# Attention of a two-layer trunk: weighted sums in unbroken blocks of five key chunks, denominators at the blocks' heads, more tiles for exponentials, TensorE in written order

## The chip, the cores and the metric

The kernel runs on one core of a Trainium2 chip. The metric is device time in microseconds (us) of one execution; the time before is the median of three runs. The profile is one further execution, recorded instruction by instruction. Its engines are PE (TensorE matmuls), PEld (TensorE weight loads), DVE (VectorE), ACT (ScalarE), POOL (GpSimd) and SP (the queue that issues DMAs).

## What is computed

Two layers over 1024 latent and 256 context tokens of width 1024, all in float32. Each layer is a token mixer and a gated feed-forward part with a convolution; layer 0 mixes by grouped-query attention with normed and rotated heads, layer 1 by latent attention. Only the attentions matter here:

```python
def attend(q, k, v):                      # layer 0, 16 heads of 64; context queries attend to context keys alone
    s = jnp.einsum('bqhgd,bkhd->bhgqk', q, k) * scale
    p = softmax_f32(s).astype(v.dtype)
    return jnp.einsum('bhgqk,bkhd->bqhgd', p, v)
...
def attend(qn, qr, kn, kr, v):            # layer 1, 16 heads, 64 + 32 wide keys
    s = (jnp.einsum('bqhd,bkhd->bhqk', qn, kn) + jnp.einsum('bqhd,bkd->bhqk', qr, kr)) * scale
    p = softmax_f32(s).astype(v.dtype)
    return jnp.einsum('bhqk,bkhd->bqhd', p, v)
```

## The kernel before

**Tiles.** Attention works on *units*: a pair of heads and 512 queries. A layer has 16 units of 10 key chunks of 128 keys. For a chunk, `scores` (L628) writes the scores of both heads, transposed (keys on partitions), into one PSUM tile `psD` of 1024 columns: four matmuls in layer 0, six in layer 1, since operands are split into a high and a low part. ACT takes their exponential into a tile `pp` (shown as `pp<-psD`, 128x1024). `weigh` (L635) multiplies it with the values and adds into a PSUM tile `psB`: one matmul for each head, 128 keys by 64 value columns, the first head's result on partitions 0 to 63 and the second's on 64 to 127 (`tp`). These are plain float32 matmuls, and the trace has two MATMUL rows for each (640 of them make its 1280 rows). The sum of exponentials, the *denominator*, is collected in a tile `acc` by 128x1024 additions on POOL; in each unit chunk 4's tile is kept aside (`PAIRS`) and added to chunk 5's tile on DVE, and POOL adds the pair. `tail` (L640) copies the weighted sum out of PSUM, multiplies `acc` with a column of ones (`psB<-s,ones`, again 64 columns for each head), takes the reciprocal on DVE and multiplies.

**Maxima.** Exponentials need a bound for each query. `unit_max` (L589) computes the scores once more with queries on partitions (per unit 16 matmuls of 512 columns and 8 of 256, `psB<-blk,s`), and DVE reduces each bank (`mx<-psB`), 24 groups in 20 steps. A small chain on DVE (`m<-mx`, `mm<-m`, `mm<-m,mm`) and eight tiny matmuls (`psB<-identb,mm`) turn the result into a row, which two ACT copies put into the operands of the unit's scores (`s<-psB 2x512`). The unit's first score can be finished only then.

**Order.** An `Emitter` (L101) keeps an estimated clock of TensorE. The main stream (scores and weighted sums) advances it; side streams (preparing operands two units ahead, maxima, tails, the second layer's modulation, context queries in layer 0) run as generators that name a time to wait before the next step. `PACE0` and `PACE1` are the waits between steps of maxima. `em.until` runs side streams alone until a condition holds, here that the next unit's row of maxima is ready. What is written in this order is then ordered anew for each engine by a scheduler, except where an engine is pinned; in the attentions none is. Each engine runs its own instructions strictly in that final order.

**The main loop** (`Attention.run`, L704). After every two chunks (`BATCH`) `flush` writes the weighted sums of two earlier chunks and, behind each, its addition to `acc`. There are four `pp` tiles, seven `s4` tiles, two `psD` tiles and four `psB` tiles. Weight tiles `whi` and `wlo` (three each) hold the split weights.

## Time and profile before

| | us |
|---|---|
| median of 3 runs (lowest, highest) | 3500.96 (3500.63, 3502.84) |
| span of the profiled execution, first to last instruction | 3497.9 |
| median less span: what lies around the span | 3.1 |
| PE busy | 3328.7 |
| DVE, POOL, ACT busy | 2198.5, 1896.6, 1518.4 |
| attention of layer 0, about | 285 to 860 |
| attention of layer 1, about | 1990 to 2650 |

A row of instruction groups has the line, engine and operation, output and inputs by the program's names, shapes and count, then busy time and mean duration in ns, then idle time before it. All compute instructions have line L159, the helper that records them, so groups are told apart by their tiles. A timeline row has start, duration, and how many equal instructions were merged in it. Matmuls overlap: a row lasts longer than the time until the next one starts, so what a matmul costs is read from start to start. The profile names tiles `s` for `s2` and `s4`.

### The profile page before, as it was taken

The numbers are of one execution on the slowest core, as the hardware profiler recorded it, in microseconds if no ns is written. First come the engines' busy times: TensorE is split into PE (matmuls) and PEld (weight loads), VectorE is DVE, ScalarE is ACT, GpSimd is POOL, SyncE is SP. The second block draws the span as 40 slices with busy tenths as digits, with TensorE's granted clock in tenths as the row PEclk, the third lists the DMA queues.
The fourth block names the chain that finished last, engine by engine and source line by source line (L and its number), as shares of the span: only waits on it lengthen the run. The fifth ranks groups of instructions, "written<-read, shape, count | busy, mean of one in ns | idle before, by whom it ended". The sixth has DMA issues, their size and how long they took to land. (4 is left out here: it accounts for less than half of the span.)

```text
span 3497.9 us, 41426 instructions
## 1 busy us (share of the span) xinstructions
PE 3328.7 (95%) x15482; PEld 2337.4 (67%) x15482; DVE 2198.5 (63%) x2619; ACT 1518.4 (43%) x2328; POOL 1896.6 (54%) x1126
## 2 busy tenths in 40 slices
PE   6999999999989999999998899999999899999988
PEld 4666444445868888878887655555557677777777
DVE  5356677774477666765845645555664766676575
ACT  4234445543254444444444434343442444444434
POOL 4324656774276666654443355555562656665455
PEclk9999999999989999999999999999999899999999
DMA  5655310000302222245231100000013122223733
GB/s 195 198 152 182 131 37 8 8 31 7 136 32 95 85 76 83 95 143 192 86 121 65 37 25 14 26 12 26 19 48 120 50 97 97 91 91 106 243 106 106
DMA packets 139049, 303.31 MB, mean 87 GB/s; under 512 B 15584, under 2 KB 35168, under 8 KB 138848
## 3 DMA queue, kind: packets, MB, share of 16 engines
q1 hardware_dynamic: 138848, 300.67, 25.5%
q8 instruction: 121, 1.98, 0.2%
q14 instruction: 80, 0.66, 0.1%
HBM read 224.85 MB, written 70.52 MB: 84 GB/s over the span
## 5 line engine op out<-in xcount | busy, mean ns | idle before, releaser
L159 DVE TENSOR_REDUCE mx<-psB 128x1 f32<-128x512 f32 (+1 forms) x640 | 431.0, 686 | 346.4 <-PE psB L159 342.3
L159 POOL TENSOR_TENSOR s<-s,pp 128x1024 f32<-128x1024 f32 x216 | 518.2, 2399 | 184.9 <-DVE pp L159 140.0
L159 ACT ACTIVATE pp<-psD 128x1024 f32<-128x1024 f32 x320 | 327.1, 1024 | 394.3 <-PE psD L159 369.3
L159 PE MATMUL psD<-s,blk 128*128 128x512 f32 (+2 forms) x1600 | 475.5, 407 | 3.9 <-POOL s L159 2.7
L159 PE MATMUL psB<-pp,blk 128*64 128x512 f32 (+2 forms) x1424 | 465.8, 592 | 0.0
L159 PEld LDWEIGHTS psD<-s,blk 128*128 128x128 f32 (+2 forms) x1600 | 291.0, 190 | 176.8 <-issue 103.1
L159 PE MATMUL psD<-blk,wh 128*128 128x512 f32 (+1 forms) x1024 | 333.8, 402 | 7.4 <-ACT blk L159 3.9
L159 DVE SCALAR_TENSOR_TENSOR s<-s,par,s 128x1023 f32<-128x1023 f32 x176 | 286.3, 1639 | 70.2 <-ACT s L159 66.7
L159 DVE TENSOR_TENSOR s<-s,s 128x512 f32<-128x512 f32 (+3 forms) x233 | 256.7, 1102 | 90.7 <-ACT s L159 79.1
L159 PE MATMUL psD<-blk,wlo 128*128 128x512 f32 (+1 forms) x1398 | 289.1, 355 | 24.8 <-POOL wlo L159 24.8
L159 POOL TENSOR_TENSOR wl<-wr,wh 128x1024 fp32r<-128x1024 f32 (+3 forms) x58 | 105.1, 1811 | 349.6 <-ACT wh L159 335.4
L159 PE MATMUL psB<-blk,s 128*128 128x512 f32 (+3 forms) x768 | 277.3, 396 | 2.5 <-DVE mx L159 1.0
L159 PEld LDWEIGHTS psD<-blk,wlo 128*128 128x128 f32 x1398 | 229.8, 190 | 72.1 <-POOL wlo L159 33.5
L159 PE MATMUL psD<-blk,pp 128*128 128x512 f32 (+1 forms) x1068 | 267.1, 394 | 11.3 <-ACT s L159 5.5
L159 PE MATMUL psB<-blk,pp 128*128 128x512 f32 x1056 | 261.6, 395 | 6.2 <-DVE s L159 2.5
L159 PEld LDWEIGHTS psB<-blk,s 128*128 128x128 f32 (+1 forms) x768 | 138.7, 190 | 192.7 <-DVE mx L159 104.1
L159 DVE TENSOR_TENSOR pp<-pp 128x512 fp32r<-128x512 f32 (+1 forms) x165 | 139.7, 851 | 182.0 <-ACT pp L159 179.9
L159 POOL TENSOR_TENSOR pp<-wraw,pp 128x512 fp32r<-128x512 f32 x88 | 144.2, 1639 | 189.8 <-ACT pp L159 181.8
L159 PEld LDWEIGHTS psD<-blk,wh 128*128 128x128 f32 (+1 forms) x1024 | 188.7, 188 | 72.9 <-issue 20.0
L159 PEld LDWEIGHTS psD<-blk,pp 128*128 128x128 f32 x1068 | 199.5, 191 | 54.6 <-ACT s L159 6.6
L159 POOL TENSOR_TENSOR s<-s,s 128x1024 f32<-128x1024 f32 (+4 forms) x72 | 142.3, 1982 | 169.8 <-ACT s L159 145.6
L159 PEld LDWEIGHTS psB<-blk,pp 128*128 128x128 f32 x1056 | 198.3, 190 | 53.4 <-DVE s L159 6.3
(156 smaller groups left out, 6195.4 us busy)
## 6 DMA issues: line engine op xcount, KB each, us to landing
pp<-g SPq DMA_DIRECT2D x143, 256.0 KB, 2.7
g<-s SPq DMA_DIRECT2D x66, 512.0 KB, 2.7
s<-in_ada_w SPq DMA_DIRECT2D x48, 512.0 KB, 6.6
blk<-in_ada_w SPq DMA_DIRECT2D x48, 512.0 KB, 5.8
wraw<-in_w_up SPq DMA_DIRECT2D x88, 256.0 KB, 2.8
pp<-in_w_up SPq DMA_DIRECT2D x88, 256.0 KB, 3.4
blk<-in_w_dn SPq DMA_DIRECT2D x86, 256.0 KB, 3.1
wr<-in_w_out SPq DMA_DIRECT2D x16, 512.0 KB, 3.7
```

Of the source, the lines that this page charges most:

```text
L159: ins = fn(*a, **k)
```

## The change

- **Blocks.** `BATCH` becomes 5, with `LEAD` 2: when seven chunks are waiting, the weighted sums of five are written in one piece. While they are written, side streams are held back (`alone`), so nothing comes between them. Denominators, and the context queries' weighted sums, are not written where their stream stands, but queued (`post`) and written ahead of the next block (`run_jobs`).
- **TensorE pinned.** During `run`, `pinned` holds "pe": TensorE keeps the written order.
- **Additions.** They are written right behind the exponential. The pair of chunks 4 and 5 is gone; instead chunk 5 is added straight to `acc` by DVE (`ACCD`). POOL has eight additions a unit, as before, and DVE one.
- **Tiles.** Exponentials use `ptile`: 12 tiles in turn in layer 0 (six `pp`, three `whi`, three `wlo`), nine in layer 1 (six `pp`, three `wlo`). For that, narrow weights of layer 1 keep both parts in one `whi` tile, and the output projection's weights of layer 0 are loaded only at the last unit. `s4` gets eight tiles. The scratch for dynamic DMAs is set to 2048.
- **Small things.** The negated maximum (`mm<-m`) goes from DVE to ACT; paces are 0.55 and 0.75; the context queries' exponentials lie in one `blk` tile.

The diff also deletes comments; that part is left out.

```diff
-TAIL_WAIT = 4.0
-PACE0 = 0.8
+PACE0 = 0.55
...
-BATCH = 2
+BATCH = 5
+LEAD = 2
...
-PACE1 = 0.9
+PACE1 = 0.75
...
-PAIRS = (4,)
+ACCD = (5,)
...
     def _run(self):
-        if self.running:
+        if self.running or self.held:
             return
...
+    @contextmanager
+    def alone(self):
+        assert not self.held
+        self.held = True
+        yield
+        self.held = False
+        self._run()
...
-        return bp.tile([P, 1024], dt, tag="s4", name=nm("s4"), bufs=7)
+        return bp.tile([P, 1024], dt, tag="s4", name=nm("s4"), bufs=8)
...
-        return bp.tile([P, 1024], dt, tag="pp", name=nm("pp"), bufs=4)
+        return bp.tile([P, 1024], dt, tag="pp", name=nm("pp"), bufs=6)
+
+    def ptile():
+        tag, pool_, n = ptags["order"][ptags["next"] % len(ptags["order"])]
+        ptags["next"] += 1
+        return pool_.tile([P, 1024], F32, tag=tag, name=nm("pt"), bufs=n)
...
-            lo = wp.tile([P, 1024], F32R, tag="wlo", name=nm("wl"))
+            if w <= 512 and order[i][0] != "m_rope":
+                hi, lo = hi[:, 0:512], hi[:, 512:1024]
+            else:
+                lo = wp.tile([P, 1024], F32R, tag="wlo", name=nm("wl"))
...
-        dve.tensor_scalar(mb[:, :w, 0], m[:, :w], -1.0, None, ALU.mult)
+        act.mul(mb[:, :w, 0], m[:, :w], -1.0)
...
+    def run_jobs():
+        while jobs:
+            jobs.pop(0)()
+
+    def post(job):
+        if gather[0]:
+            jobs.append(job)
+        else:
+            job()
...
-        yield wait
-        pss = pB()
-        for h in range(2):
-            mm(pss[64 * h:64 * h + 64, :nq], ones, acc[:, h * nq:(h + 1) * nq], tp=(0, 64 * h))
+        res = {}
+
+        def total():
+            pss = res["pss"] = pB()
+            for h in range(2):
+                mm(pss[64 * h:64 * h + 64, :nq], ones, acc[:, h * nq:(h + 1) * nq], tp=(0, 64 * h))
+
+        post(total)
+        while not res:
+            yield 0.3
+        yield 1.0
...
+            gather[0] = True
+            pinned.add("pe")
 
             def flush(n):
-                for _ in range(min(n, len(pend))):
-                    weighted(*pend.pop(0))
-
-            def weighted(u, po, pt, i, last):
-                weigh(u, po, pt, i, i == 0, last)
+                with em.alone():
+                    run_jobs()
+                    for _ in range(min(n, len(pend))):
+                        u, po, pt, i = pend.pop(0)
+                        if i == 0:
+                            po[0] = pB()
+                        weigh(u, po[0], pt, i, i == 0, i == 9)
+                        if i == 9:
+                            em.spawn(tail(u, po[0], u["acc"]))
+
+            def add(u, pt, i):
                 if i == 0:
                     u["p0"] = pt
                 elif i == 1:
                     u["acc"] = s4()
                     pool.tensor_tensor(u["acc"], u.pop("p0"), pt, ALU.add)
-                elif i in PAIRS:
-                    u["pair"] = pt
                 else:
-                    if "pair" in u:
-                        dve.tensor_tensor(pt, pt, u.pop("pair"), ALU.add)
-                    eng = dve if u is self.units[-1] and i in LASTDVE else pool
+                    eng = dve if i in (LASTDVE if u is self.units[-1] else ACCD) else pool
                     eng.tensor_tensor(u["acc"], u["acc"], pt, ALU.add)
...
                 for k in range(10):
                     S = pD()
                     scores(u, S, k)
-                    pt = pp()
+                    pt = ptile()
                     act.activation(pt, S, AF.Exp, scale=self.scale)
-                    if len(pend) == BATCH:
+                    add(u, pt, k)
+                    pend.append((u, po, pt, k))
+                    if len(pend) == BATCH + LEAD:
                         flush(BATCH)
...
+            while pend:
+                flush(BATCH)
+            pinned.discard("pe")
+            gather[0] = False
+            run_jobs()
...
+    wide_tags = [("pp", bp, 6), ("whi", wp, 3), ("wlo", wp, 3)]
+    ptags.update(next=0, order=[t for k in range(6) for t in wide_tags if k < t[2]])
     att.run(ctx_side)
```

What this does to the order is seen at three places in the later part of layer 0's attention. TensorE before, around the row of maxima of one unit: `psD` are scores, `psB_1112` is the unit's weighted sum, `pp_1135` and `pp_1144` are two chunks' exponentials, `psB_1141` and `psB_1143` are maxima, `mm` is the row.

```order
L159 MATMUL psD_1145_5287<-s4_982_4675,blk_807_3999 128x512
L159 MATMUL psD_1145_5287<-s4_983_4676,blk_806_3998 128x512
L159 MATMUL psB_1141_5273<-blk_1052_4938,s4_1062_4970 128x512
L159 MATMUL psD_1145_5287<-s4_983_4676,blk_807_3999 128x512
L159 MATMUL psB_1112_5168<-pp_1135_5251,blk_141_660 64x512
L159 MATMUL psB_1143_5282<-blk_1052_4938,s4_1062_4970 128x512
L159 MATMUL psB_1112_5168<-pp_1135_5251,blk_141_660 64x512
L159 MATMUL psB_1112_5168<-pp_1144_5285,blk_141_660 64x512 x2
L159 MATMUL psD_1155_5331<-s4_982_4675,blk_806_3998 128x512
L159 LDWEIGHTS mm_1138_5265
L159 MATMUL psB_1146_5292<-identb_77,mm_1138_5265 2x128
```

The two heads of chunk `pp_1135` stand apart, with a matmul of maxima between them. TensorE now, at the head of a block: `psB_1130` and `psB_1131` are maxima, `psB_1133` is the denominator of the unit before, `psB_1134` the weighted sum.

```order
L169 MATMUL psB_1130_5243<-blk_255_1448,blk_1112_5170 128x256 x2
L169 MATMUL psB_1131_5247<-blk_255_1448,s4_1055_4955 128x256 x2
L169 MATMUL psB_1133_5254<-s4_1050_4929,ones_79 64x512 x2
L169 MATMUL psB_1134_5257<-pt_1105_5142,blk_141_660 64x512 x2
L169 MATMUL psB_1134_5257<-pt_1108_5152,blk_141_660 64x512 x2
L169 MATMUL psB_1134_5257<-pt_1116_5184,blk_141_660 64x512 x2
L169 MATMUL psB_1134_5257<-pt_1119_5200,blk_141_660 64x512 x2
L169 MATMUL psB_1134_5257<-pt_1123_5216,blk_141_660 64x512 x2
L169 MATMUL psB_1135_5268<-blk_1044_4911,s4_1055_4955 128x512
```

Five chunks, both heads of each side by side, stand behind the denominator. TensorE now, at the end of a unit's scores: `psD_1086` is the unit's last chunk, `psB_1088` to `psB_1094` are the next unit's last maxima, `mm` its row.

```order
L169 MATMUL psD_1086_5073<-s4_923_4447,blk_255_1448 128x512
L169 MATMUL psD_1086_5073<-s4_923_4447,blk_257_1450 128x512
L169 MATMUL psB_1088_5081<-blk_798_3971,s4_979_4664 128x512
L169 MATMUL psB_1090_5089<-blk_255_1448,s4_979_4664 128x256 x2
L169 MATMUL psB_1091_5097<-blk_798_3971,s4_979_4664 128x512
L169 MATMUL psB_1092_5100<-blk_798_3971,s4_979_4664 128x512
L169 MATMUL psB_1093_5103<-blk_798_3971,s4_979_4664 128x512
L169 MATMUL psB_1094_5106<-blk_798_3971,s4_979_4664 128x512
L169 LDWEIGHTS mm_1095_5110
L169 MATMUL psB_1096_5113<-identb_77,mm_1095_5110 2x128
```

Six steps of maxima now stand together, with the row directly behind the last of them. DVE before, in a stretch with the addition of the pair (`pp_1083` and `pp_1078`) between reductions of maxima:

```order
L159 TENSOR_REDUCE mx_1047_4921<-psB_1085_5062 128x1
L159 TENSOR_REDUCE mx_1047_4921<-psB_1087_5070 128x1
L159 TENSOR_TENSOR blk_1117_5180<-blk_1116_5179,blk_1117_5180 64x256
L159 TENSOR_REDUCE mx_1047_4921<-psB_1088_5075 128x2
L159 TENSOR_TENSOR pp_1083_5057<-pp_1083_5057,pp_1078_5031 128x1024
L159 TENSOR_REDUCE mx_1047_4921<-psB_1090_5085 128x1
L159 TENSOR_REDUCE mx_1047_4921<-psB_1093_5095 128x1
L159 TENSOR_REDUCE mx_1047_4921<-psB_1095_5103 128x1
```

DVE now, around the same unit's head block as above (`s4_1109` is its `acc`, `pt_1126` its chunk 5):

```order
L169 TENSOR_REDUCE mx_1097_5124<-psB_1125_5223 128x1
L169 TENSOR_REDUCE mx_1097_5124<-psB_1128_5237 128x1
L169 TENSOR_TENSOR s4_1109_5154<-s4_1109_5154,pt_1126_5231 128x1024
L169 TENSOR_REDUCE m_1129_5242<-psB_1130_5243 128x2
L169 TENSOR_REDUCE mx_1097_5124<-psB_1131_5247 128x2
L169 RECIPROCAL s2_1139_5281<-psB_1133_5254 128x512
L169 TENSOR_REDUCE mx_1097_5124<-psB_1135_5268 128x1
L169 TENSOR_REDUCE m_1129_5242<-psB_1136_5271 128x2
```

The addition on DVE now reads and writes `acc`, which POOL has been adding to, and stands ahead of the reciprocal and of further reductions.

## The prediction

> **What bounds the kernel now.** I read the page's busy shares first, then the two attentions as windows, then TensorE's timeline inside one.

> ```profile
> PE 3328.7 (95%) x15482; PEld 2337.4 (67%) x15482; DVE 2198.5 (63%) x2619; ACT 1518.4 (43%) x2328; POOL 1896.6 (54%) x1126
> ...
> 285.00:860.00 575.00, 569.25 (x2328) 261.95 (x2327) 406.32 (x491) 278.89 (x376) 367.42 (x181) 1.00 0.17 58
> 1950.00:2645.00 695.00, 683.72 (x2787) 384.45 (x2785) 407.46 (x531) 301.44 (x417) 391.10 (x195) 0.99 0.08 27
> ```

> The columns of the windows are PE, PEld, DVE, ACT, POOL. In both attentions TensorE is idle for only 5.8 and 11.3 us; DVE is busy 71% and 59%, POOL 64% and 56%. So TensorE's own time sets the pace, and the question is how much of it is work.

> ```profile
> 598.36 0.87 PE L159 MATMUL psD<-s,blk 66*128 66x512 f32 x3
> 599.16 1.93 PE L159 MATMUL psB<-pp,blk 128*64 128x512 f32 x6
> 601.02 0.50 PE L159 MATMUL psB<-blk,s 128*128 128x256 f32 x2
> ...
> 605.24 1.07 PE L159 MATMUL psB<-pp,blk 128*64 128x512 f32 x2
> 606.24 0.50 PE L159 MATMUL psB<-blk,s 128*128 128x512 f32 x1
> 606.67 1.08 PE L159 MATMUL psB<-pp,blk 128*64 128x512 f32 x4
> 607.68 0.51 PE L159 MATMUL psB<-blk,s 128*128 128x256 f32 x2
> ...
> 609.92 1.10 PE L159 MATMUL psD<-s,blk 128*128 128x512 f32 x4
> 610.86 0.40 PE L159 MATMUL psB<-blk,s 128*128 128x512 f32 x1
> ...
> L159 PE MATMUL psB<-pp,blk 128*64 128x512 f32 x1280 | 450.1, 615 | 0.0
> L159 PE MATMUL psB<-s,ones 128*64 128x512 f32 x128 | 41.2, 614 | 0.0
> ```

> Read from start to start. One head alone (x2, two rows for a matmul) takes 606.24 - 605.24 = 1.00 us; two heads side by side (x4) take 607.68 - 606.67 = 1.01: the second is free. Three matmuls in two such turns take 601.02 - 599.16 = 1.86. So a *turn*, whether of one head or two, costs 0.86, and each block of 64-column matmuls 0.14 on top. Around it: four full matmuls take 610.86 - 609.92 = 0.94, 0.235 each, but the one between two blocks takes 606.67 - 606.24 = 0.43. So a block costs another 0.20 outside, 0.34 in all.

> **The change, TensorE's part.** Counted in the two programs' orders, layer 0 goes from 249 turns in 217 blocks to 188 in 35, layer 1 from 225 in 190 to 176 in 33. (Check: the 474 turns and 407 blocks before make 408 + 57 = 465 us. The two groups above are 491, less the 0.07 that each block's last row runs on past the next start, 28, is 463; the half-width context sums come on top.) Removed: layer 0, 61 x 0.86 + 182 x 0.34 = 114; layer 1, 49 x 0.86 + 157 x 0.34 = 96. Together 210 us, if nothing takes TensorE's place. Three small pieces cost nothing that shows: the output projection's first weights move to layer 0's last unit, over 20 us long; the feed-forward parts keep their order; more tiles only free the exponentials.

> **What becomes late.** DVE and POOL, in the order that now stands.

> ```profile
> 733.50 4.81 POOL L159 TENSOR_TENSOR s<-s,pp 128x1024 f32<-128x1024 f32 x2
> 738.39 1.06 POOL L159 TENSOR_TENSOR blk<-blk,blk 64x256 fp32r<-64x256 f32 x1
> ...
> 738.78 2.64 DVE L159 TENSOR_REDUCE mx<-psB 128x1 f32<-128x512 f32 x4
> ...
> 749.31 0.18 DVE L159 TENSOR_REDUCE m<-mx 128x8 f32<-128x24 f32 x1
> 749.52 2.35 DVE L159 TENSOR_SCALAR mm<-m 128x8 bf16<-128x8 f32 x1
> 751.91 0.17 DVE L159 SCALAR_TENSOR_TENSOR mm<-m,mm 128x8 bf16<-128x8 f32 x1
> ...
> 752.13 0.40 PE L159 MATMUL psB<-identb,mm 128*2 128x128 bf16 x8 [0.20 <-DVE mm L159]
> 752.46 0.74 PE L159 MATMUL psB<-blk,s 128*128 128x256 f32 x3
> ...
> 752.59 1.18 ACT L159 CAST s<-psB 2x512 fp32r<-2x512 f32 x2
> ...
> L159 DVE RECIPROCAL s<-psB 128x512 f32<-128x512 f32 x16 | 53.7, 3358 | 18.9 <-PE psB L159 18.9
> L159 DVE TENSOR_TENSOR s<-s,s 128x512 f32<-128x512 f32 x16 | 24.7, 1546 | 0.5
> L159 DVE TENSOR_TENSOR pp<-pp,pp 128x1024 f32<-128x1024 f32 x16 | 19.6, 1225 | 10.6 <-PE psB L159 10.6
> L159 DVE RECIPROCAL s<-psB 128x256 f32<-128x256 f32 x8 | 14.0, 1753 | 4.3 <-PE psB L159 4.3
> ...
> L159 ACT ACTIVATE pp<-psD 128x1024 f32<-128x1024 f32 x320 | 327.1, 1024 | 394.3 <-PE psD L159 369.3
> ```

> POOL adds at (738.39 - 733.50) / 2 = 2.45 apiece; queued reductions follow at about 0.62 (four in 2.64). The negated maximum cost DVE 2.35 here; on ACT I take 0.3, between the small DVE rows (0.17) and half an ACT cast of two rows (0.59).

> *A late unit of layer 0*, t = 0 at the end of its predecessor's second block. TensorE: 20 scores and nine maxima steps, 6.9; then the head block, 0.86 + 5 x 0.86 + 0.14 = 5.3, until 12.2. DVE, meanwhile: chunk 2's exponential ends at 2.7 (scores and one maximum 1.6, ACT 1.02). POOL then adds chunks 2, 3 and 4, until 10.0. Only then can DVE add chunk 5, 1.23, until 11.3; until then DVE stands still with its reductions done, and behind the addition wait two reductions (1.2) and the reciprocal (3.36), until 15.8. That is 3.6 past the block that was to hide it. Reductions for the next maxima wait in turn, and TensorE with them, for a PSUM bank. Ten more reductions (6.2), the product (1.55) and the chain to the row of maxima (0.7) end at 24.3. TensorE has long done what it can. From the row to the next unit's two first chunks: 0.33, a cast that the first head's second score waits for, eight scores, two maxima, 3.3 in all; the second block 4.4, with context sums 5.3. The unit ends at 32.9; one with a context denominator at 33.4 (1.75 more, one reduction less, no context sums). Mean 33.1.

> ```profile
> 512.30:515.70 3.40, 1.79 (x10) 1.09 (x8) 3.37 (x4) 1.43 (x2) 3.32 (x3) 1.00 0.00 0
> 515.70:519.10 3.40, 3.06 (x14) 1.53 (x14) 3.37 (x5) 1.15 (x2) 2.58 (x2) 0.51 0.40 118
> ```

> And an idle TensorE loses clock: after a stretch of 3.4 us in which it was busy 1.79, it got 0.51 for the next. The 3 us before the row of maxima bring this about in most units, and the 3.4 us after them, which all wait for, then take 1.7 longer: 0.8 x 1.7 = 1.4. So 34.5 a unit.

> [...]

> ```profile
> 330.72 0.65 PE L159 MATMUL psB<-s,ones 128*64 128x512 f32 x2
> ...
> 528.88 1.08 PE L159 MATMUL psB<-s,ones 128*64 128x512 f32 x4
> ...
> 797.70 1.08 PE L159 MATMUL psB<-s,ones 128*64 128x512 f32 x4
> ...
> 852.15 1.08 PE L159 MATMUL psB<-s,ones 128*64 128x512 f32 x4
> ...
> 2212.71 0.64 PE L159 MATMUL psB<-s,ones 128*64 128x512 f32 x1
> ...
> 2383.12 0.64 PE L159 MATMUL psB<-s,ones 128*64 128x512 f32 x1
> ...
> L159 PE MATMUL psB<-blk,sc 128*32 128x512 f32 x192 | 23.1, 598 | 0.0
> ```

> These are denominators, one a unit. Before: the next eight units (528.88 to 797.70) took 33.6 each, the first five 39.6, the last two 54.5 together. After, the eight take 34.5: +7. The first five carry the modulation's matmuls (23.1 in 12 groups, 1.9 each, mostly ahead of chunk 2) and their sums on DVE, estimated 2.5 a unit on the loop: 37.0, or -13. In the last two no maxima are left to wait for: 31.6 + 14.4 = 46, or -8. **Layer 0: -14**, between -114 (no loop) and +38 (below).

> *Layer 1* has six scores a chunk and the projections of keys and queries, so the stretch before the head block lasts 9.3, and the same chain (exponential 3.2, POOL 7.3, DVE 1.2, a reduction 0.6, reciprocal 3.4, product 1.6) ends at 17.3, the block at 14.6. TensorE then has 18 scores and n maxima, 4.2 + 0.235 n, DVE 0.62 n + 0.7. By the new order n is 6 in four units, 8 in four, 17 in three; in four more, 12 further scores stand between, and nothing waits. With 0.3 for the cast, TensorE waits 1.8, 2.6 and 6.0: 4 x 1.8 + 4 x 2.6 + 3 x 6.0 = 36. Clock after 11 waits: 11 x 0.7 x 1.7 = 13. **Layer 1: -96 + 36 + 13 = -47**, between -96 and -11 (every wait doubled). Four units before take 170.4 (2212.71 to 2383.12); after, about 158.

> Sum: -61 on a span of 3497.9, so 3437. The median stands 3.1 above the span: **3440**.

> **Rivals.**
> *TensorE stays the bound* in both layers: the order of DVE and POOL finds slack that I don't see. For it: their busy shares leave 29% and more free. Against it: additions to `acc` must follow each other. 3501 - 210 + 4 = 3295.
> *The clock holds.* Waits are cut up by scattered matmuls, so that no stretch falls below half busy. The two clock terms go: 13 x 1.4 + 13 = 31, so 3409. [...]
> *Slower: DVE locked out by POOL.*

> ```profile
> 736.24 2.62 DVE L159 TENSOR_TENSOR s<-s,s 128x512 f32<-128x512 f32 x1
> ```

> This product took 2.62, where the group's mean is 1.55; it ended 0.5 after the POOL addition that ran until 738.3. If POOL, denser now, holds up all four operations with two inputs that a unit of layer 0 has between its reductions (+1.1 for the product, +0.95, and two of up to 2 in every second unit), its loop grows by 4: 13 x 4 = 52, and layer 1's by 1.1 x 16 = 17. 3440 + 69 = 3509. It decides from 4.7 a unit over my loop in layer 0 alone, 39 us from denominator to denominator. [...]
> That blocks are broken up after all is excluded by the order.

> **How the numbers follow.** Forecast 0.55, clock holds 0.18, TensorE bound 0.07, slower 0.15, the rest (a loop half as long, near 3370) 0.05. The range leaves out TensorE's bound and the worst end of the slower case: 3385 to 3510. A measurement tells about 0.2%, 7 us, from no change. Faster: 0.07 + 0.18 + 0.05, and 0.50 of the forecast's 0.55, 0.80; within 0.2%: 0.04 of the forecast and 0.03 of the slower case, 0.07; slower 0.13.

> **What would show it.** The group of 64-column matmuls near 330 us busy in place of 491; PE's share of the attentions down to three quarters in layer 0; DVE idle there "<-POOL s" before 128x1024 additions; granted clock below 1.00 in layer 0's windows; denominators 34 to 35 us apart late in layer 0. I am wrong if PE stays above 95% busy there, or if those denominators stand under 30 us apart.

## The result, and the profile after

| | before | after |
|---|---|---|
| median, us | 3500.8 | 3519.8 |
| lowest and highest of 4 runs | 3498.5, 3502.8 | 3516.7, 3525.7 |
| ratio after/before, 95% interval | | 1.006, 1.0046 to 1.0075 |
| span of the profiled execution | 3497.9 | 3514.9 |

The change makes the kernel 0.6% slower. The forecast was 3440, with a range from 3385 to 3510: wrong in sign, and outside the range.

First the busy shares of the page, then the two attentions as windows (columns PE, PEld, DVE, ACT, POOL, granted clock, DMA share, GB/s), each from its first score to the last 64-column matmul.

```profile
PE 3216.1 (91%) x15482; PEld 2390.5 (68%) x15482; DVE 2175.3 (62%) x2577; ACT 1524.5 (43%) x2368; POOL 1914.3 (54%) x1128
```

```profile
284.00:896.30 612.30, 518.74 (x2279) 284.34 (x2277) 387.08 (x464) 283.04 (x399) 374.92 (x182) 0.89 0.16 55
2027.80:2673.20 645.40, 599.81 (x2642) 391.69 (x2642) 352.89 (x462) 283.02 (x393) 381.47 (x188) 0.93 0.08 26
```

TensorE is busy 113 us less, and the program still takes longer: it stands idle for 93.6 us of layer 0's attention and 45.6 of layer 1's, and where it works it gets 0.89 and 0.93 of its clock (before 1.00 and 0.99). The groups of 64-column matmuls, by shape:

```profile
L169 PE MATMUL psB<-pt,blk 128*64 128x512 f32 x1280 | 291.1, 601 | 0.0
L169 PE MATMUL psB<-s,ones 128*64 128x512 f32 x128 | 34.4, 615 | 0.2
```

They are 325.5 in place of 491.3. What TensorE waits for in layer 0's attention, before and then after (us in total, times, longest):

```profile
PE psB L159 <- DVE mm L159: 3.3, 7, 2.0
PE psD L159 <- ACT pp L159: 1.2, 1, 1.2
```

```profile
PE psB L169 <- DVE mm L169: 48.2, 14, 5.6
PE psB L169 <- DVE s L169: 23.3, 13, 2.2
PE psB L169 <- DVE mx L169: 8.7, 16, 0.9
PE psD L169 <- ACT pt L169: 5.6, 7, 2.1
```

The first is the wait for the row of maxima, the second the wait for the PSUM bank that the reciprocal reads. In layer 1 the row alone takes 38.2 (the first line below). The other two lines are DVE's wait for POOL's additions in layer 0, before and then after:

```profile
PE psB L169 <- DVE mm L169: 38.2, 12, 8.7
...
DVE s L159 <- POOL s L159: 2.5, 1, 2.5
...
DVE s L169 <- POOL s L169: 49.8, 16, 4.2
```

Here is the second wait, on DVE and then on TensorE, in one unit of layer 0:

```profile
801.24 1.23 DVE L169 TENSOR_TENSOR s<-s,pt 128x1024 f32<-128x1024 f32 x1 [3.15 <-POOL s L169]
802.38 0.68 DVE L169 TENSOR_REDUCE m<-psB 128x2 f32<-128x512 f32 x1
802.98 0.68 DVE L169 TENSOR_REDUCE mx<-psB 128x2 f32<-128x512 f32 x1
803.58 3.35 DVE L169 RECIPROCAL s<-psB 128x512 f32<-128x512 f32 x1
```

```profile
804.11 0.63 PE L169 MATMUL psD<-s,blk 128*128 128x512 f32 x2
806.98 0.58 PE L169 MATMUL psB<-blk,s 128*128 128x512 f32 x1 [2.24 <-DVE s L169]
807.36 1.48 PE L169 MATMUL psD<-s,blk 128*128 128x512 f32 x3
808.64 0.63 PE L169 MATMUL psB<-blk,s 128*128 128x512 f32 x1
```

DVE waits 3.15 us for POOL's chain, adds chunk 5, does two reductions, and only then the reciprocal; TensorE gets the bank when that ends. Behind the wait three scores take 1.28 us from start to start (808.64 - 807.36), at a granted clock of 1.00 three take 0.71 (846.12 to 846.83): the granted clock is 0.50 here (second window below). The unit's row of maxima brings a second wait. Windows of 3.41 us, laid on the stretches of the granted clock (in both traces each recorded stretch but the last is a whole number of these windows, 1 to 219):

```profile
803.84:807.25 3.41, 1.17 (x6) 0.73 (x6) 3.41 (x2) 0.00 (x0) 1.13 (x1) 1.00 0.00 0
807.25:810.66 3.41, 3.41 (x9) 2.66 (x9) 2.77 (x5) 1.31 (x3) 1.04 (x1) 0.50 0.00 0
810.66:814.08 3.42, 2.40 (x13) 1.36 (x12) 3.42 (x5) 2.38 (x3) 3.34 (x2) 1.00 0.00 0
814.08:817.49 3.41, 2.33 (x11) 1.37 (x10) 2.48 (x5) 2.05 (x6) 3.41 (x3) 1.00 0.00 0
817.49:820.90 3.41, 2.43 (x14) 1.98 (x15) 1.51 (x2) 1.22 (x3) 2.12 (x2) 0.50 0.02 5
820.90:824.32 3.42, 3.42 (x10) 2.25 (x10) 1.38 (x2) 1.19 (x2) 0.00 (x0) 0.50 0.00 0
824.32:827.73 3.41, 3.41 (x22) 1.37 (x20) 0.00 (x0) 1.23 (x2) 2.35 (x1) 1.00 0.00 0
```

One unit, two losses of clock, and the second lasts two windows, the first of them busy 2.43 of 3.41. Over both attentions there are 33 such stretches of half clock, 9 of one window, 16 of two and 8 of three, against three before (one of them in layer 0).

**Where the time went.** The span is split at the first score and the last 64-column matmul of each attention. *Idle* is time without a row of TensorE; *clock* is busy time multiplied by one less the granted clock; *work* is the rest.

| after less before, us | length | work | idle | clock |
|---|---|---|---|---|
| ahead of layer 0's attention | -3.2 | -2.2 | -0.8 | -0.1 |
| layer 0's attention | +46.9 | -90.6 | +87.9 | +49.6 |
| between the attentions | +16.1 | +12.3 | +5.6 | -1.7 |
| layer 1's attention | -37.2 | -110.0 | +38.7 | +34.1 |
| behind it | -5.5 | +0.2 | -1.6 | -4.1 |

The 16.1 between the attentions is no loss of its own: maxima and projections of layer 1's first units (26 and 57 matmuls) now stand ahead of its first score, so layer 1 is judged by the two rows together, -21.1.

### The profile page after: what moved, and what is told of

It reads as the page before. It is cut to its first block, busy times and chain, and to the rows that moved or that the text cites. A ratio compares the mean times of both kernels' runs of the same rounds, so it can differ in the third digit from the quotient of the medians.

```text
span 3514.9 us, 41287 instructions
## 1 busy us (share of the span) xinstructions
PE 3216.1 (91%) x15482; PEld 2390.5 (68%) x15482; DVE 2175.3 (62%) x2577; ACT 1524.5 (43%) x2368; POOL 1914.3 (54%) x1128
## 3 DMA queue, kind: packets, MB, share of 16 engines
q1 hardware_dynamic: 138848, 300.67, 25.6%
## 5 line engine op out<-in xcount | busy, mean ns | idle before, releaser
L169 POOL TENSOR_TENSOR s<-s,pt 128x1024 f32<-128x1024 f32 x218 | 519.7, 2384 | 210.2 <-ACT pt L169 163.9
L169 PE MATMUL psD<-s,blk 128*128 128x512 f32 (+2 forms) x1600 | 498.1, 428 | 10.8 <-ACT pt L169 10.4
L169 ACT ACTIVATE pt<-psD 128x1024 f32<-128x1024 f32 x320 | 326.3, 1024 | 311.1 <-PE psD L169 302.1
L169 PEld LDWEIGHTS psD<-s,blk 128*128 128x128 f32 (+2 forms) x1600 | 321.4, 207 | 94.5 <-ACT pt L169 23.7
L169 PE MATMUL psB<-blk,s 128*128 128x512 f32 (+3 forms) x768 | 290.1, 416 | 36.4 <-DVE s L169 21.2
L169 DVE TENSOR_TENSOR s<-s,s 128x512 f32<-128x512 f32 (+3 forms) x233 | 239.5, 1029 | 123.2 <-ACT s L169 108.6
L169 PE MATMUL psB<-pt,blk 128*64 128x512 f32 x1280 | 291.1, 601 | 0.0
L169 PE MATMUL psD<-blk,pp 128*128 128x512 f32 (+1 forms) x1068 | 268.6, 395 | 20.1 <-ACT pp L169 11.3
L169 PEld LDWEIGHTS psB<-blk,s 128*128 128x128 f32 (+1 forms) x768 | 153.4, 209 | 148.5 <-issue 48.8
L169 PEld LDWEIGHTS psD<-blk,wh 128*128 128x128 f32 (+1 forms) x1024 | 188.1, 188 | 74.0 <-issue 16.1
L169 POOL TENSOR_TENSOR whi<-blk,whi 128x512 fp32r<-128x512 f32 x97 | 145.8, 1504 | 122.9 <-ACT whi L169 121.1
```

The source lines that it names most:

```text
L169: ins = fn(*a, **k)
```

## The experiments

The questions: is it the waits themselves or the clock behind them (A and B), DVE and POOL being simply full (C), the pin (D), or the length of a block? Ratios are to the kernel before; the change itself stands at 1.006.

| kernel | median, us | ratio, 95% interval | half-clock stretches, layers 0 + 1 |
|---|---|---|---|
| first addition on DVE | 3496.0 | 0.9998, 0.9988 to 1.0007 | 19 + 12 |
| ten extra matmuls | 3506.8 | 1.0024, 1.0013 to 1.0036 | 18 + 5 |
| first addition, five extra matmuls | 3472.7 | 0.9932, 0.9918 to 0.9947 | 16 + 5 |
| block ahead of the row | 3472.8 | 0.9935, 0.9913 to 0.9958 | 20 + 9 |
| closer maxima | 3478.9 | 0.9945, 0.993 to 0.996 | 17 + 11 |
| no pin | 3426.0 | 0.9795, 0.9779 to 0.9811 | 10 + 3 |
| before, with the pin alone | 3525.4 | 1.008, 1.0064 to 1.0097 | 7 + 3 |
| blocks of two | 3423.1 | 0.979, 0.9775 to 0.9804 | 13 + 3 |
| blocks of two, first addition | 3414.7 | 0.9762, 0.9746 to 0.9778 | 13 + 3 |
| both repairs, blocks 5, 5 | 3382.4 | 0.9669, 0.9653 to 0.9685 | 7 + 4 |
| both repairs, blocks 3, 3, 4 | 3371.2 | 0.9637, 0.9622 to 0.9651 | 6 + 2 |
| both repairs, blocks 2, 2, 2, 4 | 3359.7 | 0.9609, 0.9594 to 0.9623 | 4 + 0 |

### DVE's wait for POOL: the first addition on DVE

```diff
-ACCD = (5,)
+ACCD = ()
-                    pool.tensor_tensor(u["acc"], u.pop("p0"), pt, ALU.add)
+                    dve.tensor_tensor(u["acc"], u.pop("p0"), pt, ALU.add)
```

> The change, with the unit's first addition (chunks 0 and 1) on DVE in place of chunk 5's; POOL keeps eight additions. DVE's addition then waits for two exponentials only, never for POOL. Theory A (DVE's in-order queue is held by POOL's chain of additions, TensorE then waits for a PSUM bank, and the clock halves): in layer 0 the 49.8 us of DVE waiting for POOL and TensorE's 23.3 us for the reciprocal's bank go, about ten of the 21 half-clock stretches go with them: 40 us less than the change, near 3480. Rival C (DVE and POOL are simply full, the loop is their sum): the waits move elsewhere, within 7 us of 3520.

Measured: 0.6% less than the change, 22 to 24 us, all of it in layer 0 (585.1 for its attention in place of 612.3; layer 1 645.4 and 645.5). DVE's wait for POOL and TensorE's wait for the reciprocal's bank are gone. C falls. But only two of the 21 half-clock stretches went, not ten: the waits for the row (54.0 now, 48.2 in the change) and for exponentials (15.4, 5.6 in the change) are left.

### The clock by itself: extra matmuls ahead of the row

```diff
         pr = pB()
+        for _ in range(FILL if full else 0):
+            pe.matmul(pr, u["aq"][0][:, 0:P], u["ak"][0][:, 0:512], start=True, stop=True)
```

> The change, with ten extra matmuls of 512 columns (2.4 us at full clock) on TensorE between the last maxima and the row of maxima; they compute scores that the row then overwrites. Theory B (the idle time itself is cheap, what costs is the half clock behind it): the stretches at half clock fall from 33 in the two attentions to 15 or fewer, the 85 us of clock loss there to about 45, and after some 15 us for the units where nothing was waited for, the time is near 3495. Theory A without B (after the wait everything hangs on DVE again, and a slow TensorE is hidden): 0 to 20 us more than the change, 3520 to 3540.

Measured: 0.4% less than the change with ten matmuls. Clock loss in the attentions went from 90.2 to 60.5, idle time from 139.2 to 73.2, and the fillers added 75.8 of work. This program computes more, to no use, and is faster: 3506.8 in place of 3519.8. TensorE's order in the attentions is otherwise the same: set against each other, the two traces differ by 31 insertions of ten matmuls and nothing else, so it is no new order that gained the time. B holds, at about half of what was expected: the waits for the reciprocal's bank are left (23.4 us), as are 18 of layer 0's 21 clock stretches. So the same again, smaller and without those waits:

> The change with the first addition on DVE (3496 alone; 54.0 and 38.0 us of TensorE waiting for the row, 31 half-clock stretches in the attentions) and five extra matmuls (1.2 us) ahead of the row. Where TensorE waits 3.4 us for the row, they lie inside the wait and delay nothing; where it doesn't, they cost 1.2 us, in some five units 6 us. If the half clock behind the waits costs what its rows show (86 us in the attentions): stretches fall to about 15, and the time to 3460. If it is hidden behind DVE: 3496 to 3502.

Measured: 3472.7, 23 us less than without the fillers. Idle time in the attentions fell by 38.5 (121.9 to 83.4), work rose by 44.4, and clock loss fell by 31.0 (86.0 to 55.0). Filler and idle time nearly cancel (5.9 more of the two together); what the program gained, 23 to 25 us, is the clock. The expected 3460 was not reached since 21 stretches stayed, not 15.

### The row of maxima: a block ahead of it

```diff
+        u["maxed"] = True
         yield u.get("wait", MROW_WAIT)
...
+                em.until(lambda: "maxed" in u)
+                if len(pend) >= BATCH:
+                    flush(BATCH)
                 em.until(lambda: "ready" in u)
```

> The change, with the second block of a unit's weighted sums moved: written between the next unit's last maxima and its row of maxima, in place of behind the next unit's first two chunks. The block (4.4 to 5.3 us) then covers the chain on DVE from the last reductions to the row. Theory A: TensorE's waits for that chain (48.2 us in layer 0, 38.2 in layer 1) go nearly all, and the half-clock stretches behind them: 110 to 130 us less than the change, near 3400. Rival C (DVE and POOL full): the waits come back elsewhere, 3490 to 3520.

Measured: 1.2% less than the change, between the two expectations and nearer the rival's. TensorE's waits in layer 0 of this kernel:

```profile
PE psD L169 <- ACT pt L169: 31.9, 32, 3.8
PE psB L169 <- DVE s L169: 18.1, 12, 2.8
PE psB L169 <- DVE mx L169: 16.0, 31, 2.0
PE psD L169 <- ACT s L169: 7.5, 11, 4.1
PE psB L169 <- DVE mm L169: 1.0, 1, 1.0
```

The wait for the row is gone (1.0 of 48.2), but in layer 0 others took its place: DVE now waits 72.8 us for POOL (49.8 before), and scores wait for exponentials. In layer 1 the repair alone brings 27.6 us (617.9 in place of 645.5). In layer 0 it brings 18 (594 in place of 612), and the first one alone had brought 27. Both together, blocks still of five:

> The change with both repairs, the block ahead of the row (3473 alone) and the first addition on DVE (3496 alone), blocks still of five. If the two waits were the whole of the matter (blocks of five cost nothing by themselves): 3390 or less, since 57 blocks fewer than in the version with blocks of two and four (3360) save 19 us. If the block's length is a cause of its own (DVE has no maxima to reduce for 4.4 us, and they come in a heap behind it): 3420 to 3450.

Measured: 3382.4, below 3390 as the first reading has it. The two repairs alone brought 0.6 and 1.2%; together they bring 3.9%, since each had uncovered the other's wait: in layer 0 the row's is 1.0 us now and DVE's for POOL 2.1, and its attention takes 538, 74 less than in the change.

### The heap of maxima: closer steps

```diff
-PACE0 = 0.55
+PACE0 = 0.2
-PACE1 = 0.75
+PACE1 = 0.35
```

> The change (blocks of five) with the steps of maxima written closer: PACE0 0.2 and PACE1 0.35 in place of 0.55 and 0.75. A unit's maxima are then written out several scores ahead of its row, and no heap of them stands in front of the row. Theory A1 (what costs is the heap of maxima at the unit's end with the row right behind it, not the length of the block): TensorE's 86 us of waits for that chain fall below 20, half-clock stretches from 33 to 15, the time to 3430 to 3450. Theory A2 (the block itself costs, since DVE gets nothing to reduce for 4.4 us and is late ever after): the wait goes from the row to the banks of the maxima (TensorE waiting for the reductions), and the time stays at 3490 or above.

Measured: between the two again. Waits for the row fell from 86.4 to 25.6 us, but TensorE now waits 35.1 for reductions (9.3 before), and DVE for POOL 57.1 in layer 0. Neither A1 nor A2 alone.

### The length of a block

Blocks of two, in the change and nothing else:

```diff
-BATCH = 5
+BATCH = 2
```

> The change with BATCH 2: blocks of two chunks, 163 blocks in the two attentions in place of 68. If TensorE's blocks cost what was worked out (0.34 us each), 95 more cost 32 us of TensorE, of which a part fills waits: 3520 to 3550. If the length of the blocks is what makes the waits (maxima held back for 4.4 us at a time, then in a heap), waits and half-clock stretches fall and the time is below the change's, 3480 or less.

Measured: 2.7% less than the change, though TensorE has 95 blocks more to switch for. The second reading holds. Layer 1 nearly loses its waits (idle 11.8, clock 9.5); layer 0 keeps 37.1 us for the row. With the first repair:

> Blocks of two (3423 alone) and the unit's first addition on DVE in place of chunk 5's. With blocks of five this brought 0.6%, all of it in layer 0, where DVE waited 49.8 us for POOL; with blocks of two that wait is 21.0 us. If the two gains add by that wait: 8 to 12 us, near 3412. If the shorter block had already taken away what the wait costs: no change, 3423.

Measured: 8 to 10 us less, as expected from the 21.0 us, though the intervals overlap by a hair. With both repairs, LEAD 4 and everything pending written ahead of the row (`flush(len(pend))`):

> Blocks of two with the first addition on DVE, LEAD 4, and whatever is pending (four chunks, 3.6 us) written between the next unit's last maxima and its row. Of the 3423 of blocks of two alone, TensorE's waits for the row are 45.5 us, its clock loss in the attentions 38.8. Theory A: most of both goes, and 38 blocks fewer than with blocks of two save 13: near 3350. Rival (as with blocks of five and the moved block, where waits for exponentials and banks took their place): 3390 to 3420.

Measured: 3359.7, nearer to Theory A's 3350 than to the rival's 3390; 4% less than the kernel before, and the best version. Its two attentions as windows:

```profile
285.00:804.00 519.00, 486.46 (x2270) 254.21 (x2268) 401.06 (x465) 280.56 (x399) 375.96 (x180) 0.98 0.19 65
1940.00:2517.00 577.00, 570.25 (x2644) 363.21 (x2644) 376.34 (x463) 283.87 (x393) 378.63 (x187) 1.00 0.09 29
```

TensorE's timeline in two late units of its layer 0, 30.7 us apart (before about 33.6, in the change 37.8): the block of four chunks, and the row behind it.

```profile
642.11 3.65 PE L169 MATMUL psB<-pt,blk 128*64 128x512 f32 x16
646.01 0.40 PE L169 MATMUL psB<-identb,mm 128*2 128x128 bf16 x8 [0.25 <-DVE mm L169]
...
672.81 3.65 PE L169 MATMUL psB<-pt,blk 128*64 128x512 f32 x16
...
677.08 0.40 PE L169 MATMUL psB<-identb,mm 128*2 128x128 bf16 x8
```

In these two units the block covers DVE's chain, and TensorE waits 0.25 us for the row or nothing; in all of layer 0 it waits 6.7 us for it. Longer blocks with the same repairs, `LEAD` 3:

> Both repairs with blocks of three, three and four chunks (100 blocks in place of 125 in the version at 3360). 25 blocks fewer are 8 us of TensorE; if no new wait comes: 3350. If longer blocks bring waits in the measure of their length: 3360 to 3380.

Measured: 3371.2, as the second reading has it: slower than 2, 2, 2, 4 though it has 25 blocks fewer; with 5, 5 it is 3382.4. The intervals of the first two touch (0.9622 and 0.9623), but no run of one (3367.3 to 3372.2) lies among those of the other (3358.8 to 3363.4). From 125 blocks to 68, the switches saved would be worth 19 us at 0.34 each, and 23 are lost. So longer blocks cost by themselves as well, with one reservation: the three versions also differ in `LEAD` (4, 3 and 2), and in whether all that is pending or five chunks go ahead of the row; no run changes the length alone.

### The pin

The change without the line that pins TensorE:

```diff
-            pinned.add("pe")
```

> The change without the pin: the scheduler orders TensorE's instructions anew, as before the change; blocks are then broken up to 156 in place of 68, which costs 30 us of TensorE. Rival D (the written order is what makes TensorE wait, a scheduler would put scores between the maxima and the row): waits for the row fall by half or more, and the time is 3440 to 3480. Otherwise (DVE's own order makes the waits, whatever TensorE's is): 3520 to 3550.

Measured: 2.6% less than the change, more than D expected. In layer 0:

```profile
PE psB L169 <- DVE s L169: 25.4, 15, 2.3
PE psB L169 <- DVE mm L169: 9.2, 11, 2.9
```

The wait for the bank is as it was, that for the row falls from 48.2 to 9.2 (in layer 1 from 38.2 to 6.0): the scheduler puts other matmuls between the last maxima and the row (in layer 1 five to 18 rows in every unit, where the change has none to two in 12 of 15), at the price of 88 blocks. Is it the pin by itself? The kernel before with the pin:

> The kernel before with TensorE pinned to its written order in the attentions, and nothing else of the change. If the pin makes the waits by itself: waits for the row of maxima rise from 7.6 us to 40 or more, half-clock stretches appear, 1.01 to 1.02 of the time before. If the pin only costs together with long blocks (in the old written order a score or a sum stands between the last maxima and the row in most units): waits under 15 us, within 0.3% of before.

Measured: 0.8% slower than before, between the two expectations. Waits for the row are 16.8 us, ten half-clock stretches appear. The pin costs some 28 us in the old order with its short blocks, and 94 in the new order: it does harm by itself, and more together with long blocks.

## Why the prediction was wrong, step by step

| sum over both attentions and what lies between, us | forecast | measured |
|---|---|---|
| TensorE's work | -210 | -188 |
| idle | +82 + 36 = +118 | +132 |
| clock | +18 + 13 = +31 | +82 |
| rest of the program | 0 | -9 |
| sum | -61 | +17 |

The 82 of idle time is what the forecast's -14 for layer 0 leaves after -114 of work and 18 of clock.

- **The step that failed is the clock term**: "in most units, and the 3.4 us after them, which all wait for, then take 1.7 longer: 0.8 x 1.7 = 1.4". It took one loss of clock a unit, and one window for each. In the eight units from 533.69 to 836.19 there are 13 stretches at half clock (1.6 a unit), 6.3 us each on the mean (81.9 in all), and the clock costs 31.6 / 8 = 4.0 a unit. The units take 37.8, not 34.5; 2.6 of these 3.3 us are the clock. In the whole of layer 0 the term was short by 32, in layer 1 by 19: together 51 of the 78 us that the forecast missed. That lost clock was lost time here the fillers show: 31.0 us less of it, and 23 us less time.
- Both halves of the mistake were in view. The wait for the reciprocal's bank was in my loop ("TensorE with them, for a PSUM bank"), but I gave only the wait for the row a loss of clock. And I had looked at when the clock falls, not at when it comes back: in the traces of before and after, no window at half clock in which TensorE was busy below 0.8 was followed by one at full clock (0 of 46).
- By stage, layer 0 took 8.0 us more than before up to the first denominators (the forecast has no term there), 0.5 more in the next five units (forecast -13), 33.7 more in the eight behind them (+7) and 4.5 more from there on (-8). So the loop of late units is not the only part that came out too long.
- **The work** was right in layer 1 (-96; measured -110.0 + 12.3 = -97.7) and 23 short in layer 0. The blocks themselves save what was said (325.5 us for the two groups, "near 330"). Most of the rest is probably wait that is recorded as work. At the wait that ends at 845.79, the matmul ahead of it is recorded for its full 0.40 us, where in a stream the next would start after 0.24, and the one behind it takes 0.33 until the next start: together some 0.25 of busy time without work. Counting every gap, however short, layer 0 has 97 in place of 18: 79 x 0.25 = 20. That is worked out, not tried.
- **The idle time** was near in both layers: 82 forecast and 87.9 in layer 0, 36 and 38.7 + 5.6 in layer 1. DVE does wait for POOL ahead of the addition (49.8 us, 16 times), and the reciprocal does end late. One term of it was too small, the chain on DVE to the row; the last rival below has it.
- *TensorE stays the bound* and *the clock holds* fell: TensorE stands idle for 93.6 and 45.6 us, and 33 stretches at half clock came. That the clock holds while no stretch is below half busy was my guess, and no run shows it: the stretch in front of the one at 0.51 was itself busy 1.79 of 3.40, 0.53, and of the windows at full clock that were busy 0.4 to 0.8, in before and after, 32 of 145 were followed by half clock.
- *Slower: DVE locked out by POOL* has the sign of the result but not its main cause. The product, whose price it raised, takes 0.68 in layer 0 now, where it took 1.55. But DVE lost time beside POOL at another place, on the way to the row of maxima: in the instruction `mm<-m,mm` that ends DVE's chain. The first two rows below are before, the others after; the two last are one unit, on DVE and on POOL:

```profile
L159 DVE SCALAR_TENSOR_TENSOR mm<-m,mm 128x8 bf16<-128x8 f32 x15 | 7.1, 475 | 0.5
L159 DVE SCALAR_TENSOR_TENSOR mm<-m,mm 128x4 bf16<-128x4 f32 x8 | 1.2, 155 | 0.0
...
L169 DVE TENSOR_TENSOR s<-s,s 128x512 f32<-128x512 f32 x16 | 10.9, 680 | 0.1
L169 DVE SCALAR_TENSOR_TENSOR mm<-m,mm 128x8 bf16<-128x8 f32 x15 | 12.6, 840 | 3.9 <-ACT mm L169 3.8
L169 DVE SCALAR_TENSOR_TENSOR mm<-m,mm 128x4 bf16<-128x4 f32 x8 | 10.3, 1288 | 0.0
...
817.60 0.82 DVE L169 SCALAR_TENSOR_TENSOR mm<-m,mm 128x8 bf16<-128x8 f32 x1 [0.43 <-ACT mm L169]
...
816.04 2.35 POOL L169 TENSOR_TENSOR s<-s,pt 128x1024 f32<-128x1024 f32 x1
```

Over both layers 21 of its 32 rows of 128x8 take more than 0.4 us, up to 2.3; each of the 21 starts while a POOL row runs and ends 0.02 to 0.03 us behind it (here at 818.42 and 818.39). The other 11 take 0.16 to 0.17. Why is not shown. The forecast had 0.17 for it and 0.7 for the whole chain behind the reductions; here that chain runs from 816.99 to 818.42, 1.43. Before, it was the negation that took long (1.48 on the mean in layer 0; over both layers 24 of its 32 rows of 128x8 over 0.4, each ending 0.03 to 0.04 behind a POOL row); on ACT it takes 0.21, and the next instruction takes 0.84 in layer 0 in place of 0.48. At 0.87 on the mean in place of 0.17, 32 times, that is at most 22 us of TensorE's 86 for the row: an estimate, no run tries it.

- Of the signs listed, the groups' time, the granted clock below 1.00 and the idle "<-POOL s" came. PE's share in layer 0 is 0.85, not three quarters: busy time at a slow clock counts in it (without the clock loss it is 0.76). The forecast's own terms would have made it (569.25 - 114 + 18) / (575 - 14) = 0.84, so three quarters did not follow from them. Denominators late in layer 0 stand 37 to 41 us apart, not 34 to 35, which is the clock term again. Neither of the two signs of being wrong came, since both look for a loop that is faster than forecast, and this one was slower.
- Two readings of the forecast are off without consequence: four reductions in 2.64 are 0.66 apart, not 0.62 (in the change they stand 0.60 apart, 802.38 to 802.98), and a unit with a context denominator comes by its own terms to 33.1, not 33.4.

Open: how the harm divides between the pin and the block. Each taken away alone brings some 95 us (3426.0 and 3423.1), so they act together; no run has blocks of five kept whole, without the pin. The tiles and the negation on ACT were not taken away by themselves either.

## What to carry to other kernels

When work is taken from the busiest engine, write down what it will wait for next, and put something between the last producer and the row that everything hangs on; here a block of sums moved by a few lines turned 0.6% loss, with a second repair, into a gain of 3 to 4%. Price an idle gap by the clock that follows it as well: until when it is down, and how often in a loop (here 4.0 us a unit, where the forecast had 1.4). A longer block was not the better one here: 3382.4 with 5, 5 and 3371.2 with 3, 3, 4, against 3359.7 with 2, 2, 2, 4, though `LEAD` differs as well.
